# Reciprocal roots of the norms by one GpSimd power, weight splits and normed rows moved between VectorE, ScalarE and GpSimd, in a transformer of two parts on one core

## The chip, the cores and the metric

The kernel runs on one core of one Trainium2 chip. A core has five engines with queues of their own: PE (TensorE, matrix products), DVE (VectorE), ACT (ScalarE), POOL (GpSimd) and SP (SyncE, which here only issues loads). The metric is the time of one execution on the device in microseconds (us), lower is better; the median of the runs is compared.

## The reference

256 tokens of width 1024 go through two blocks. The first has two layers, each a feed-forward, a mixer of four attentions and a second feed-forward, with a layer norm behind each. The second has a convolution, an attention and two expert layers, with root-mean-square norms between them. Cut to what the change touches:

```python
def layer_norm(x, g, b):
    mu = jnp.mean(x, -1, keepdims=True)
    var = jnp.mean(jnp.square(x - mu), -1, keepdims=True)
    return (x - mu) * lax.rsqrt(var + LN_EPS) * g + b

def rms_norm(x, g):
    return x * lax.rsqrt(jnp.mean(x * x, -1, keepdims=True) + RMS_EPS) * g

for l in range(2):
    x = layer_norm(ALPHA * x + 0.5 * swiglu(x, ffn1...), ln1_g[l], ln1_b[l])
    x = layer_norm(ALPHA * x + hybrid_mixer(x, w_in[l], ...), ln2_g[l], ln2_b[l])
    x = layer_norm(ALPHA * x + 0.5 * swiglu(x, ffn2...), ln3_g[l], ln3_b[l])
# second block
h = h + conformer_conv(rmsnorm(h, a_norm_g))        # with a layer norm inside
h = h + peer(rmsnorm(h, f_norm_g[0]))
h = h + diff_attention(rmsnorm(h, b_norm_g), ...)   # with an rmsnorm for each of 8 heads
h = h + peer(rmsnorm(h, f_norm_g[1]))
out = rmsnorm(h, final_norm_g)
```

Each mixer has a norm of its inputs `mla_norm` and one behind each of its four groups.

## The kernel before

Activations lie transposed, features on the 128 partitions and tokens along the row, in tiles of 128x256. Every product with large weights is made of three matmuls, `mm3`: a number is split into a rounded high part and the rest (`wh` and `wl` of the weights, `xh` and `xl` of the activations), and high x high, low x high and high x low are summed in PSUM.

`weights` streams weights from DRAM through a ring: SP loads 128x1024 (`w`, four buffers), ACT rounds 128x512 of it to `wh` (L396), and the engine named by the string `self.lo` subtracts it, `wl = w - wh` (L398): `v` is DVE, `g` POOL, and longer strings are cycled. `wh` and `wl` have six buffers each; one feeds four steps of twelve matmuls. A buffer comes free when PE has done with it, so ACT's and DVE's or POOL's next instruction waits on PE, and PE on them.

A layer norm is put off. `project` leaves the unnormed rows (`x`, and `z` scaled by the gain) and their sums. The next stage starts with products on the unnormed `z` (its *head*: six chunks of the mixer's input, or four pairs of a feed-forward), and behind the first of them `factors` makes the norm: PE sums over the features (L300, L301), DVE makes mean and variance (L304 to L306), `newton` the reciprocal root, DVE the shift (L308), and PE spreads both over the partitions by transposes (`spread`, L445). PE's rows run in one order, so it stands at the spread until `newton` is done. Then `finish` makes the normed rows chunk by chunk, eight chunks: DVE multiplies and adds (L324, L325), ACT makes `xh` (L328) while POOL makes `x` (L329) from the same `lnt`, and DVE makes `xl` of both (L330). `newton` is eleven small DVE instructions, each reading the one before: two integer steps (L434, L435) and three rounds of three (L437 to L439).

It is called 30 times: in six layer norms' `factors`, in two `mla_norm`, eight `group_out` (behind each of a mixer's groups), five `rms_factor`, one in `conformer` and eight in the attention's heads (`step_N`).

The strings are `HEAD_LO = 'g'` (the heads of mixers and feed-forwards), `MIX_LO` and `OUT_LO` `'ggv'` (the rest of a mixer, and its output product), `'v'` for feed-forwards. The second block has strings of its own, in which POOL has most splits.

The order of instructions on each engine is set when the kernel is built, by a scheduler that follows a model of the times; engines then run their rows strictly in that order.

Of the kernel before, what the change touches and what calls it, by code (L numbers as in the profile page):

```python
# [15 lines left out]
U32 = mybir.dt.uint32  # L16
I32 = mybir.dt.int32
AF = mybir.ActivationFunctionType
ALU = mybir.AluOpType
# [12 lines left out]
HEAD_LO = 'g'  # L32
HEAD_AT = 1
MIX_LO = ('ggv', 'ggv')
OUT_LO = ('ggv', 'ggv')
# [249 lines left out]
class Rows:  # L285
# [8 lines left out]
    def factors(self, k):  # L294
# [12 lines left out]
        r = k.newton(v)  # L307
# [7 lines left out]
    def finish(self, k):  # L315
# [6 lines left out]
        for c in range(DC):  # L322
            q = k.tl(k.w1, [128, T], "lnt")
            nc.vector.tensor_tensor(q, xp[:, c], ps[:, 0], op=ALU.mult)  # L324
            nc.vector.tensor_tensor(q, q, ps[:, 1], op=ALU.add)  # L325
            if self.out is None:
                h, l = [a[:, :T] for a in self.xs[c]]
                nc.scalar.activation(h, q, AF.Identity, bias=b[:, c:c + 1], scale=g[:, c:c + 1])  # L328
                nc.gpsimd.tensor_scalar(o[:, c], q, g[:, c:c + 1], b[:, c:c + 1], op0=ALU.mult, op1=ALU.add)  # L329
                nc.vector.tensor_tensor(l, o[:, c], h, op=ALU.subtract)  # L330
            elif LN_H[c] == "s":
                nc.scalar.activation(o[:, c], q, AF.Identity, bias=b[:, c:c + 1], scale=g[:, c:c + 1])
            else:
                nc.gpsimd.tensor_scalar(o[:, c], q, g[:, c:c + 1], b[:, c:c + 1], op0=ALU.mult, op1=ALU.add)
# [12 lines left out]
class Kernel:  # L347
    def __init__(self, ctx, nc, tc, I):
# [9 lines left out]
        nc.vector.memset(self.ones, 1.0)  # L358
        self.col = self.tl(gp, [128, 3], "col")
# [69 lines left out]
    def newton(self, v):  # L429
# [3 lines left out]
        a = self.tl(self.wk, [128, 8], "na", bufs=4)[:v.shape[0], :v.shape[1]]  # L433
        nc.vector.tensor_scalar(y.bitcast(U32), v.bitcast(U32), 1, None, op0=ALU.logical_shift_right)  # L434
        nc.vector.tensor_scalar(y.bitcast(I32), y.bitcast(I32), -1.0, float(0x5f3759df), op0=ALU.mult, op1=ALU.add)  # L435
        for _ in range(3):
            nc.vector.tensor_tensor(a, v, y, op=ALU.mult)  # L437
            nc.vector.scalar_tensor_tensor(a, a, -0.5, y, op0=ALU.mult, op1=ALU.mult)
            nc.vector.scalar_tensor_tensor(y, a, 1.5, y, op0=ALU.add, op1=ALU.mult)  # L439
# [294 lines left out]
    def group_out(self, grp, o):  # L734
# [9 lines left out]
        r = self.newton(ss)  # L744
# [80 lines left out]
    def mla_norm(self, x):  # L825
# [16 lines left out]
        r = self.newton(t)  # L842
# [356 lines left out]
    def rms_factor(self, s2, t0):  # L1199
# [15 lines left out]
        r = self.newton(v)  # L1215
# [6 lines left out]
    def conformer(self, z, ss):  # L1222
# [62 lines left out]
        r = self.newton(v)  # L1285
# [29 lines left out]
    def attention(self, zk, ss):  # L1315
# [104 lines left out]
        def step_N(hd, n):  # L1420
# [8 lines left out]
            r = self.newton(q)  # L1429
# [289 lines left out]
```

## Time and profile before

| | us |
|---|---|
| median of three runs | 3370.47 |
| the three runs | 3356.43, 3370.47, 3370.92 |
| profiled execution | 3374.15 |
| its span, first to last instruction | 3372.3 |
| PE, DVE, ACT, POOL busy | 3205.0, 2399.8, 1650.9, 1190.2 |
| mean granted clock of PE | 0.963 |

PE is busy for 95% of the span, so the reading starts at PE's waits and at the stretches where its clock was granted at half. The first block takes the first 1230 us: feed-forward, mixer, feed-forward up to 625 us, and the same again. A head follows at about 200, 420, 625, 826 and 1035 us.

### The profile page before, as it was taken

How to read it: one execution, taken by the hardware profiler on the slowest of the kernel's cores; microseconds unless marked ns; L12 is line 12 of the kernel's file. 1: busy time of each engine (PE TensorE's matmuls, PEld its weight loads, DVE VectorE, ACT ScalarE, POOL GpSimd, SP SyncE). 2: the span in 40 equal slices, each digit the busy share in tenths (PEclk: the TensorE clock that was granted, in tenths of full speed). 3: DMA queues.
4: the chain of work that ended last, by engine and by line, in shares of the span. 5: the costliest groups of instructions: out<-in, count | busy, mean ns of one | idle time of the engine just before them, and what ended most of it. 6: DMA issues, size and time to landing. Idle time of an engine off the chain costs nothing.

```text
span 3372.3 us, 70124 instructions
## 1 busy us (share of the span) xinstructions
PE 3205.0 (95%) x27035; PEld 3082.0 (91%) x27035; DVE 2399.8 (71%) x5664; ACT 1650.9 (49%) x3361; POOL 1190.2 (35%) x958
## 2 busy tenths in 40 slices
PE   8989999999999999879999999999988999999998
PEld 8987799999778988879999999999887999999898
DVE  5666576766658579893797548956899397755965
ACT  5555355555535552545444454455454545445444
POOL 0053220303413000565444444344357544444443
PEclk9998799999889999989999999999998999999999
DMA  7642156565205653335444554454344545455454
GB/s 240 183 144 91 45 163 181 165 190 171 82 32 160 184 171 127 121 119 163 151 157 140 168 175 143 141 174 157 102 132 131 185 152 172 156 177 170 132 182 138
DMA packets 140863, 503.16 MB, mean 149 GB/s; under 512 B 17328, under 2 KB 19632, under 8 KB 139888
## 3 DMA queue, kind: packets, MB, share of 16 engines
q1 hardware_dynamic: 137104, 496.06, 46.6%
q8 instruction: 212, 3.47, 0.4%
q10 hardware_dynamic: 3328, 2.36, 0.2%
q14 instruction: 123, 1.01, 0.1%
q0 software_dynamic: 96, 0.26, 0.0%
HBM read 496.36 MB, written 1.05 MB: 147 GB/s over the span
## 4 chain that ended last, share of the span: by engine, by line
PE 51%; DVE 17%; issue 2%; ACT 0%; POOL 0%; DMA 0%; SPq 0%; DVEq 0%; ACTq 0%; POOLq 0%
PE A L420 7%; PE A L421 7%; PE A L422 7%; PE D L420 7%; PE D L422 7%; PE D L421 7%; DVE A L1503 2%; DVE two L1498 2%; DVE wl L398 1%; PE C L1507 1%; PE B L1246 1%; PE C L420 1%; PE C L421 1%; PE C L422 1%; DVE room L1604 1%
## 5 line engine op out<-in xcount | busy, mean ns | idle before, releaser
L396 ACT ACTIVATE wh<-w 128x512 fp32r<-128x512 f32 x1856 | 1152.9, 626 | 1313.7 <-PE A L421 513.4
L398 POOL TENSOR_TENSOR wl<-w,wh 128x512 fp32r<-128x512 f32 x774 | 1069.4, 1389 | 1622.5 <-ACT wh L396 1167.9
L398 DVE TENSOR_TENSOR wl<-w,wh 128x512 fp32r<-128x512 f32 x1082 | 764.3, 708 | 522.4 <-ACT wh L396 482.1
L420 PE MATMUL A<-xh,wh 128*128 128x256 f32 (+2 forms) x1912 | 558.8, 294 | 21.3 <-ACT wh L396 8.7
L421 PE MATMUL A<-xl,wh 128*128 128x256 f32 (+2 forms) x1912 | 556.6, 292 | 9.3 <-DVE xl L330 5.8
L422 PE MATMUL A<-xh,wl 128*128 128x256 f32 (+2 forms) x1912 | 555.1, 291 | 2.8 <-POOL wl L398 2.8
L420 PE MATMUL D<-xh,wh 128*128 128x256 f32 (+2 forms) x1664 | 481.3, 289 | 4.8 <-ACT wh L396 4.4
L422 PE MATMUL D<-xh,wl 128*128 128x256 f32 (+2 forms) x1664 | 477.9, 287 | 7.2 <-DVE wl L398 4.2
L421 PE MATMUL D<-xl,wh 128*128 128x256 f32 (+2 forms) x1664 | 477.9, 287 | 2.1 <-DVE xl L330 2.0
L420 PEld LDWEIGHTS A<-xh,wh 128*128 128x128 f32 x1912 | 370.4, 194 | 25.6 <-ACT wh L396 8.9
L421 PEld LDWEIGHTS A<-xl,wh 128*128 128x128 f32 x1912 | 371.5, 194 | 12.6 <-DVE xl L330 8.0
L422 PEld LDWEIGHTS A<-xh,wl 128*128 128x128 f32 x1912 | 372.6, 195 | 3.8 <-POOL wl L398 3.4
L421 PE MATMUL A<-rr,wh 128*128 128x272 f32 (+1 forms) x1152 | 333.4, 290 | 2.3 <-DVE rr L1196 2.2
L422 PE MATMUL A<-rr,wl 128*128 128x272 f32 (+1 forms) x1152 | 334.2, 290 | 1.1 <-POOL wl L398 1.1
L420 PE MATMUL A<-rr,wh 128*128 128x272 f32 (+1 forms) x1152 | 333.8, 290 | 0.0
L420 PE MATMUL D<-rr,wh 128*128 128x272 f32 (+1 forms) x1152 | 333.4, 289 | 0.0
L422 PE MATMUL D<-rr,wl 128*128 128x272 f32 (+1 forms) x1152 | 333.3, 289 | 0.0
L421 PE MATMUL D<-rr,wh 128*128 128x272 f32 (+1 forms) x1152 | 331.9, 288 | 0.0
L422 PEld LDWEIGHTS D<-xh,wl 128*128 128x128 f32 x1664 | 317.9, 191 | 9.7 <-DVE wl L398 5.6
L420 PEld LDWEIGHTS D<-xh,wh 128*128 128x128 f32 x1664 | 317.9, 191 | 6.7 <-ACT wh L396 5.5
L421 PEld LDWEIGHTS D<-xl,wh 128*128 128x128 f32 x1664 | 317.9, 191 | 3.4 <-DVE xl L330 3.1
L421 PEld LDWEIGHTS A<-rr,wh 128*128 128x128 f32 x1152 | 220.2, 191 | 2.8 <-DVE rr L1196 2.7
(482 smaller groups left out, 6775.2 us busy)
## 6 DMA issues: line engine op xcount, KB each, us to landing
w<-in_u_dram SPq DMA_DIRECT2D x256, 512.0 KB, 3.5
w<-in_v_dram SPq DMA_DIRECT2D x256, 512.0 KB, 3.8
w<-in_ffn_w_dram SPq DMA_DIRECT2D x240, 512.0 KB, 4.1
w<-in_win_f_dram SPq DMA_DIRECT2D x32, 512.0 KB, 3.6
w<-in_f_wq_dram SPq DMA_DIRECT2D x32, 512.0 KB, 3.5
w<-in_ffn_w_dram SPq DMA_DIRECT2D x32, 384.0 KB, 3.2
w<-in_pw_dram SPq DMA_DIRECT2D x24, 512.0 KB, 3.7
w<-in_w_out_dram SPq DMA_DIRECT2D x16, 512.0 KB, 3.7
```

The source lines that it names most:

```text
L396: nc.scalar.activation(h, s, AF.Copy)
L398: (nc.vector if eng == "v" else nc.gpsimd).tensor_tensor(l, s, h, op=ALU.subtract)
L420: mm(ps, wh, xh, start=start, stop=False)
L421: mm(ps, wh, xl, start=False, stop=False)
L422: mm(ps, wl, xh, start=False, stop=stop)
L1246: mm(pc, d[:, k], u[:, k:k + T2], start=k == 0, stop=k == n - 1)
L1498: nc.vector.tensor_tensor(two, self.key[:, None].to_broadcast([128, 4, 128, 2]), row(1, 128), op=ALU.is_equal)
L1503: nc.vector.tensor_tensor(A[:, i], one, row(2 + i, n), op=ALU.mult)
L1507: mm(ps[:, k], two[:, k // 2, :, k % 2], A[:, i, k // 2, :, k % 2], start=i == 0, stop=i == 1)
L1604: nc.vector.tensor_tensor(c[:, o:o + (b - a) * n].rearrange("p (a b) -> p a b", b=n), r.v[0][:, hd, a:b][:, :, None].to_broadcast([128, b ...
```

## The change

`newton` becomes `rsqrt`, one POOL instruction, `v ** -0.5` against a small constant tile. In the heads, in mixers and their output products all splits `wl` are made by DVE. In `finish`, ACT makes `x` (with gain and bias) and then `xh` as a rounded copy of it; POOL has nothing to do there. Lines from 358 on move by up to four.

```diff
-HEAD_LO = 'g'
+HEAD_LO = 'v'
-MIX_LO = ('ggv', 'ggv')
-OUT_LO = ('ggv', 'ggv')
+MIX_LO = ('v', 'v')
+OUT_LO = ('v', 'v')
...
-        r = k.newton(v)
+        r = k.rsqrt(v)
...
-                nc.scalar.activation(h, q, AF.Identity, bias=b[:, c:c + 1], scale=g[:, c:c + 1])
-                nc.gpsimd.tensor_scalar(o[:, c], q, g[:, c:c + 1], b[:, c:c + 1], op0=ALU.mult, op1=ALU.add)
+                nc.scalar.activation(o[:, c], q, AF.Identity, bias=b[:, c:c + 1], scale=g[:, c:c + 1])
+                nc.scalar.activation(h, o[:, c], AF.Copy)
                 nc.vector.tensor_tensor(l, o[:, c], h, op=ALU.subtract)
...
+        self.half = self.tl(gp, [128, 8], "half")
+        nc.gpsimd.memset(self.half, -0.5)
...
-    def newton(self, v):
+    def rsqrt(self, v):
         y = self.tl(self.wk, [128, 8], "ny", bufs=4)[:v.shape[0], :v.shape[1]]
-        a = self.tl(self.wk, [128, 8], "na", bufs=4)[:v.shape[0], :v.shape[1]]
-        nc.vector.tensor_scalar(y.bitcast(U32), v.bitcast(U32), 1, None, op0=ALU.logical_shift_right)
-        nc.vector.tensor_scalar(y.bitcast(I32), y.bitcast(I32), -1.0, float(0x5f3759df), op0=ALU.mult, op1=ALU.add)
-        for _ in range(3):
-            nc.vector.tensor_tensor(a, v, y, op=ALU.mult)
-            nc.vector.scalar_tensor_tensor(a, a, -0.5, y, op0=ALU.mult, op1=ALU.mult)
-            nc.vector.scalar_tensor_tensor(y, a, 1.5, y, op0=ALU.add, op1=ALU.mult)
+        nc.gpsimd.tensor_tensor(y, v, self.half[:v.shape[0], :v.shape[1]], op=ALU.pow)
         return y
```

The built programs show how rows move. First DVE in the head of layer 0's mixer, from the statistics of the layer norm on (`lnst`); before, with the first round of `newton` (`ny`, `na`):

```order
L304 COPY lnst_2638<-B_2633 128x4
L305 TENSOR_TENSOR lnst_2638<-lnst_2638 128x2
L306 SCALAR_TENSOR_TENSOR lnst_2638<-lnst_2638 128x2
L434 TENSOR_SCALAR ny_2642<-lnst_2638 128x2
L435 TENSOR_SCALAR ny_2642<-ny_2642 128x2
L437 TENSOR_TENSOR na_2643<-lnst_2638,ny_2642 128x2
L438 SCALAR_TENSOR_TENSOR na_2643<-na_2643,ny_2642 128x2
L439 SCALAR_TENSOR_TENSOR ny_2642<-na_2643,ny_2642 128x2
```

and after, on DVE at the same place:

```order
L400 TENSOR_TENSOR wl_2763<-w_2760,wh_2762 128x512
L304 COPY lnst_2640<-B_2635 128x4
L305 TENSOR_TENSOR lnst_2640<-lnst_2640 128x2
L306 SCALAR_TENSOR_TENSOR lnst_2640<-lnst_2640 128x2
L400 TENSOR_TENSOR wl_2767<-w_2760,wh_2766 128x512
L308 SCALAR_TENSOR_TENSOR lnst_2640<-lnst_2640,ny_2644 128x2
L400 TENSOR_TENSOR wl_2798<-w_2795,wh_2797 128x512
```

Before, two more rounds of three and L308 follow with no split between; now splits stand around the statistics, and L308 waits for POOL's `ny` with splits behind it.

POOL at that place; before, the last splits of the head alternate with the normed rows:

```order
L398 TENSOR_TENSOR wl_2811<-w_2804,wh_2810 128x512
L398 TENSOR_TENSOR wl_2917<-w_2914,wh_2916 128x512
L329 TENSOR_SCALAR x_1758<-lnt_2840,vec_6_93 128x256
L398 TENSOR_TENSOR wl_2954<-w_2951,wh_2953 128x512
L329 TENSOR_SCALAR x_1758<-lnt_2846,vec_6_93 128x256
```

and after, on POOL (`ISA` is the configuration of POOL's code; before it stands ahead of POOL's first split):

```order
L991 COPY acc_2879<-const_97 128x128 x2
L435 ISA
L435 TENSOR_TENSOR ny_2644<-lnst_2640,half_69 128x2
L601 TENSOR_TENSOR turn_2889<-turn_2889,const_97 128x256
L602 TENSOR_TENSOR m_478_2888<-m_478_2888,turn_2889 128x256
L890 TENSOR_TENSOR z_3480<-m_478_2888,small_101 64x240
```

POOL has no split left in the head: the power stands alone between the mixer's constants and the first rotary product.

DVE at the mixer's `mla_norm` (`mst` is its sum), before:

```order
L434 TENSOR_SCALAR ny_3038<-mst_3036 128x4
L398 TENSOR_TENSOR wl_3194<-w_3191,wh_3193 128x512
L603 STREAM_SHUFFLE turn_3065<-p_3057 128x256
L604 TENSOR_TENSOR iq_522_3064<-p_3057,const_95 128x256
L435 TENSOR_SCALAR ny_3038<-ny_3038 128x4
L437 TENSOR_TENSOR na_3039<-mst_3036,ny_3038 128x4
L398 TENSOR_TENSOR wl_3292<-w_3285,wh_3291 128x512
```

and after, on DVE:

```order
L837 TENSOR_SCALAR mst_3027<-D_3020 128x4
L344 TENSOR_TENSOR p_3037<-p_3037,lnt_3040 128x256
L400 TENSOR_TENSOR wl_3174<-w_3171,wh_3173 128x512
L599 STREAM_SHUFFLE turn_3045<-p_3037 128x256
L600 TENSOR_TENSOR iq_521_3044<-p_3037,const_97 128x256
L400 TENSOR_TENSOR wl_3178<-w_3171,wh_3177 128x512
L840 TENSOR_SCALAR mrq_3031<-ny_3029 128x2
```

Before, other work stands between the steps of `newton`; now only the use of its result (L840) is left, behind two splits and the rotary steps.

On PE, the number of matmuls between a norm's sums and its spread falls: from 49 to 37 in the mixers' heads (to 40 in the feed-forwards' heads), and from 62 to 31 in `mla_norm`. PE's rows also shift by a few places within the mixers, the conformer and the attention; in the feed-forwards behind their heads and in both expert layers behind their routing they stand as before. On SP two loads change places. POOL has 644 splits instead of 774, DVE 1212 instead of 1082; from the first of the expert layers on, `wl` is made where it was.

## Rows read from the trace of the kernel before

**Rows 1.** Page, part 1: busy us (share of the span) and instructions

```profile
PE 3205.0 (95%) x27035; PEld 3082.0 (91%) x27035; DVE 2399.8 (71%) x5664; ACT 1650.9 (49%) x3361; POOL 1190.2 (35%) x958
```

**Rows 2.** Waits of PE, whole run: us in total, times, longest us

```profile
PE B L445 <- DVE ny L439: 26.4, 10, 4.4
...
PE A L421 <- DVE xl L330: 5.8, 7, 1.1
...
PE B L300 <- DVE s L586: 3.3, 2, 1.9
PE A L421 <- DVE xl L580: 3.2, 2, 1.6
...
PE B L445 <- DVE cst L1286: 3.0, 1, 3.0
PE A L420 <- ACT sb L594: 3.0, 2, 1.5
```

**Rows 3.** Timeline of DVE, first layer norm: start, us, instruction

```profile
207.81 1.22 DVE L434 TENSOR_SCALAR ny<-lnst 128x2 uint32<-128x2 uint32 x1
...
214.02 0.16 DVE L439 SCALAR_TENSOR_TENSOR ny<-na,ny 128x2 f32<-128x2 f32 x1
```

**Rows 4.** Timeline of POOL in the same head

```profile
203.97 7.61 POOL L398 TENSOR_TENSOR wl<-w,wh 128x512 fp32r<-128x512 f32 x6
...
219.82 1.30 POOL L398 TENSOR_TENSOR wl<-w,wh 128x512 fp32r<-128x512 f32 x1 [2.73 <-ACT wh L396]
221.10 0.56 POOL L329 TENSOR_SCALAR x<-lnt,vec 128x256 f32<-128x256 f32 x1
```

**Rows 5.** Timeline of DVE, the last layer norm, POOL idle

```profile
1227.85 0.17 DVE L434 TENSOR_SCALAR ny<-lnst 128x2 uint32<-128x2 uint32 x1
...
1229.82 0.16 DVE L439 SCALAR_TENSOR_TENSOR ny<-na,ny 128x2 f32<-128x2 f32 x1
```

**Rows 6.** Timeline of DVE, layer 0's `mla_norm`

```profile
246.01 0.16 DVE L434 TENSOR_SCALAR ny<-mst 128x4 uint32<-128x4 uint32 x1
...
255.64 0.16 DVE L439 SCALAR_TENSOR_TENSOR ny<-na,ny 128x4 f32<-128x4 f32 x1
```

**Rows 7.** Splits, line 398, POOL (196 to 420 us), DVE (465 to 600): ns min/median/max

```profile
L398 POOL TENSOR_TENSOR wl<-w,wh x46: 1090/1292/2095, 195.8 to 418.6; 128x512 fp32r<-128x512 f32 x43, 128x424 fp32r<-128x424 f32 x3
...
L398 DVE TENSOR_TENSOR wl<-w,wh x97: 417/693/695, 465.1 to 599.4; 128x512 fp32r<-128x512 f32 x91, 128x256 fp32r<-128x256 f32 x6
```

**Rows 8.** Stretches: us; PE, PEld, DVE, ACT, POOL busy (instructions); PE's clock; DMA

```profile
400.00:425.00 25.00, 21.21 (x154) 20.40 (x153) 22.10 (x36) 14.35 (x31) 18.62 (x13) 0.91 0.45 137
425.00:465.00 40.00, 36.35 (x271) 35.04 (x270) 33.00 (x84) 26.42 (x51) 16.85 (x16) 0.93 0.49 145
```

**Rows 9.** Short stretches behind PE's waits at a spread, columns as before

```profile
215.60:219.00 3.40, 3.40 (x18) 3.40 (x17) 3.24 (x9) 1.12 (x2) 0.55 (x1) 0.50 0.07 6
219.00:222.40 3.40, 3.40 (x31) 3.40 (x30) 1.76 (x8) 2.60 (x5) 2.58 (x3) 1.00 0.40 122
256.50:263.30 6.80, 6.80 (x28) 4.90 (x27) 3.16 (x8) 3.72 (x6) 1.89 (x3) 0.50 0.25 78
...
1038.20:1041.60 3.40, 3.40 (x17) 3.40 (x18) 1.89 (x9) 1.23 (x2) 0.00 (x0) 0.50 0.09 34
```

**Rows 10.** Groups by line, whole run: busy us, mean ns, idle before

```profile
L329 POOL TENSOR_SCALAR x<-lnt,vec 128x256 f32<-128x256 f32 x40 | 33.7, 844 | 24.4 <-DVE lnt L325 20.3 <-PE A L421 3.5 <-PE A L422 0.5
...
L412 ACT ACTIVATE hh<-silu 128x256 fp32r<-128x256 f32 x88 | 35.5, 404 | 3.1 <-DVE silu L549 3.0
```

**Rows 11.** Groups of POOL by line and shape, whole run, columns as before

```profile
L605 POOL TENSOR_TENSOR turn<-turn,const 128x256 f32<-128x256 f32 x20 | 15.6, 778 | 28.4 <-DVE turn L603 28.4
...
L406 POOL COPY const<-silu 128x1 f32<-128x1 f32 x2 | 0.4, 187 | 93.2 <-DVE silu L549 93.2
```

**Rows 12.** Line 398 at 70 to 80 us: POOL's configuration, ns min/median/max

```profile
L398 POOLq MODIFY_POOL_CONFIG  x2: 1/3/5, 73.4 to 73.5; - x2
```

**Rows 13.** Waits of PE, 1380 to 2600 us, columns as in rows 2

```profile
PE B L445 <- DVE ny L439: 2.5, 2, 1.8
```

More of the change, by code (lines that the diff above doesn't have):

```diff
@@ L743, in group_out @@
         nc.vector.tensor_scalar(ss, ss, 1.0 / 256, 1e-6, op0=ALU.mult, op1=ALU.add)
-        r = self.newton(ss)
+        r = self.rsqrt(ss)
         y = self.tl(self.mx, [128, 2, T], "y", bufs=2)
@@ L841, in mla_norm @@
         nc.vector.tensor_scalar(t, st, 1e-6, None, op0=ALU.add)
-        r = self.newton(t)
+        r = self.rsqrt(t)
         rq = self.tl(mx, [128, 2], "mrq")
@@ L1214, in rms_factor @@
         nc.vector.tensor_scalar(v, st, 1e-6, None, op0=ALU.add)
-        r = self.newton(v)
+        r = self.rsqrt(v)
         ps = self.bank("B", T2 - t0)
@@ L1284, in conformer @@
         nc.vector.scalar_tensor_tensor(v, e2, 1e-6, v, op0=ALU.add, op1=ALU.subtract)
-        r = self.newton(v)
+        r = self.rsqrt(v)
         nc.vector.scalar_tensor_tensor(nmr, mean, -1.0, r, op0=ALU.mult, op1=ALU.mult)
@@ L1428, in step_N @@
             nc.vector.scalar_tensor_tensor(q, ss, 1.0 / 128, q, op0=ALU.mult, op1=ALU.add)
-            r = self.newton(q)
+            r = self.rsqrt(q)
             o = new_o()
```

## Prediction

> **What bounds the kernel now.** I read the page first: PE is busy 95% of the span [rows 1], so nothing is to be had but from PE's waits and from stretches in which its clock is granted at half. The view of PE's waits comes next. Its longest line is the spread of a norm's factors, which waits for `newton` on DVE: 26.4 us in ten waits, and 3.0 us in the conformer's norm (cst) [rows 2]. The waits for the splits of normed rows (xl L330), for an evacuation behind them (sb), and for the sums and splits of the mixer's output product (s L586, xl L580) are 5.8, 3.0, 3.3 and 3.2 us.
>
> The timelines tell why `newton` is slow. With POOL idle its eleven steps take 1227.85 to 1229.98, 2.1 us [rows 5]. In the first layer norm they take 207.81 to 214.18, 6.4 us: steps on two numbers per partition that last 0.16 or 0.17 us there last 1.2 us here [rows 3], and just then POOL has six splits in a row [rows 4] of 1.3 us each. So a small DVE step waits for a whole POOL split, again and again. In `mla_norm` it is 246.01 to 255.80, 9.8 us [rows 6]. Behind a wait PE pays once more: in 215.6 to 219.0 its clock is granted at 0.50 (1.2 GHz) and 18 matmuls run, in the next 3.4 us at 1.00 (2.4 GHz) 31 [rows 9].
>
> **The change part by part.** *The power.* It takes eleven DVE steps out and puts one POOL step on 2 to 4 numbers per partition in, with a hand-over to POOL and one back. No row shows a power. Below it is bounded by POOL's copy of one column, 0.19 us, and by a two-input POOL instruction of 256 columns, 0.78 us [rows 11], of 512 columns 1.29 us [rows 7]: a line through these two meets zero columns at 0.27 us. Above there is no row, since a power may be a long routine; I bound it by what `newton` took at its worst, 9.8 us. I take 1.0 us: nearest to the copy and the 0.27 us, with room for the function itself and for waiting behind a DVE split of 0.69 us [rows 7], which now stands beside it on DVE. The price moves nothing while it is covered. PE has 37 matmuls between sums and spread in a mixer's head, 40 in a feed-forward's; at 31 in 3.4 us [rows 9] that is 4.1 and 4.4 us. The chain in it is three small DVE steps, the power and L308, 0.8 us and the power; so a power of up to 3.3 us stops nobody. In `mla_norm` 31 matmuls give 3.4 us against 0.2 us and the power: up to 3.2 us.
>
> Ten plus one waits are 29.4 us [rows 2]. Three stand where PE has nothing between sums and spread (the last layer norm, the conformer, the final norm), and POOL is idle there: each waits about as long as `newton` and the steps around it, some 2.7 us by [rows 5] and 3.0 in the conformer's row, together 8.4 us, and each gains 2.1 - 1.0 - 0.2 for two hand-overs = 0.9, **-2.8 us**. Of the other eight, 21 us, two (2.5 us [rows 13]) are before expert layers, where POOL's queue is full of splits and the power stands among them: half of it goes. Six are in heads and `mla_norm` and are covered, 18.5 us. Together **-20 us**. In the mixers' groups and the attention's heads a shorter root lies beside other matmuls of PE; I count nothing there. In the attention the power is queued between the two rotary steps of a key on POOL (L1341, L1342), so the key waits for it; a step of 1 us ahead of the next scores is covered by the products of the same head, and costs up to 8 x 1 us if it is not.
>
> *The clock.* Five stretches at half clock follow those six waits, from 215.6 (3.4 us) and 256.5 (6.8 us) to 1038.2 us (3.4 us), 24 us in all [rows 9]. At half clock half is lost, 12 us, if PE had matmuls ready; behind `mla_norm` (28 matmuls in 6.8 us) it partly had not. **-8 us**.
>
> *The splits.* 130 of 128x512 go from POOL to DVE. On DVE one lasts 0.69, on POOL 1.29 us [rows 7], so DVE gets 90 us over both layers and loses 16 times `newton` of the first block, and the stretching. Whether it fits is seen in the tightest stretch, the output product: DVE is busy 22.1 of 25.0 us there and POOL's 13 splits would add 9.0 [rows 8], 6 us too many if DVE's own steps stay as they are. But part of these 22.1 us is waiting for POOL as in rows 3: eight steps stretched by some 0.7 to 1.1 us would make the room. In the next head it is 33.0 of 40 and eight of POOL's 16 instructions are splits (the others are L329), 8 x 0.69 = 5.5 [rows 8], which fits. I take that the waits for s L586 and xl L580, 6.5 us [rows 2], lose 2.5, **-2.5 us**, and that the fuller, single DVE queue gives new waits of 1 us in each of five heads and one more in the output products: **+6 us**. Behind L308, which waits for the power, splits stand in DVE's queue; six buffers of splits hold them off PE.
>
> *The normed rows.* POOL's 40 steps of 0.84 us (L329) go; ACT gets 40 rounded copies, 0.40 us each [rows 10], 16 us in all, beside PE. For one chunk `xl` now comes behind two ACT steps, where before ACT and POOL ran side by side: some 0.2 us later, but the whole row of chunks starts 4 to 6 us earlier. Of the waits for xl L330 and sb, 8.8 us [rows 2], I take half, **-5 us**, and **+1 us** for ACT.
>
> The sum: -20 - 2.8 - 8 - 2.5 + 6 - 5 + 1 = -31 us on the profiled execution of 3374.15 us (span 3372.3): 3343. That execution lies 3.7 us above the median of the runs; against the median, 3370.5, I say 3341.
>
> One rule of the Trainium skill speaks against the power. POOL switches from a split to a TENSOR_SCALAR within 0.02 us [rows 4], and its configuration row takes 5 ns, over 100 us ahead of the head's splits [rows 7, 12]; no row here shows a load of code. The skill (GPSIMD Engine Reference, Instruction dispatch) says that the first call of a freshly loaded kernel pays about 6 us (5.95 measured) that no instruction shows; paid once it would make the first head's spread some 1 us late, the sum -30, and paid at each return to the power it is the slow power below.
>
> **The rivals.** *More of the clock* (14%): in the mixers PE's matmuls follow short DVE and ACT steps in turn, and their clock is granted at half, as in 256.5 to 263.3, where 28 run in 6.8 us [rows 9]. Without POOL's splits these steps are shorter. If six more such stretches over both mixers come at full clock, that is 6 x 3.4 = 20 us more: 3321. Against it: no row shows PE waiting there by name.
>
> *DVE becomes the bound* (16%): the stretching is not given back, since DVE's splits now stand in front of the same small steps. Then the two output products lack 6 us each, the five heads behind layer norms some 2 us each, half of the clock's 8 us comes, and nothing of the -5, -2.5 and +6: -20 - 2.8 - 4 + 12 + 10 = -5, 3366 against the median. For it: the 22.1 of 25 us; against it: one split is half as long on DVE as on POOL.
>
> *The waits go, the clock does not* (6%): the half-clock stretches come behind whatever short wait is next. -31 + 8 + 4 = -19: 3352.
>
> *A slow power* (7%), the one that ends slower. If one takes 6 us, the six covered places wait 6 x 2.7 = 16 us, about what they waited; the three bare ones lose 4.1 each, 12 us; the eight groups of the mixers, with half of 3.9 us each on the way, 16 us; and nothing of the clock or the chunks is gained. About +25: 3396. It decides from about 4.5 us on, where 6 x 1.2 + 3 x 2.6 + 8 x 1.2 = 25 us eat what the sum gains from the waits and half of the rest. For it only that no row excludes it; against it that POOL's rows grow by 2 ns a column [rows 7, 11] and this has two to four.
>
> *The roots are no bound* would be the case where the change does not do what it says; the ten waits exclude it, as each names `newton`.
>
> **How the numbers follow.** The forecast, 3341, has 57%. Its own bounds: with the power at 0.3 us and all of the half-clock 12 us back, 3334; with a power at 3 us (3 x 2 us more) and +12 of new waits, 3353. A range that leaves out the slow power and the outer half of the clock's rival is 3315 to 3367; it takes in DVE as the bound. 0.5% is about what a measurement of this kernel can tell from no change, 17 us: faster is below 3353.6. To it go the forecast, the clock's rival and half of the third (57 + 14 + 3) and a little of DVE's (2): 76%. Within 0.5%: 14 + 3 = 17%. Slower: 7%.
>
> **What would show it.** In the profile of the changed kernel: PE's wait for `ny` at the spread below 8 us in total, and only where PE has nothing between; a POOL row of 128x2 of about 1 us; DVE's L305, L306, L308 at 0.16 us; no half clock at 215.6 and 256.5; DVE in the output product at 20 to 23 of 25 us. It is wrong if POOL's 128x2 row lasts over 3.3 us, if PE's waits for `wl` and `xl` from DVE grow by more than 12 us, or if the granted clock of the mixers' middle falls.

## The result

| | before | after |
|---|---|---|
| median of the runs, us | 3365.65 | 3312.70 |
| all runs, us | 3356.43 to 3370.92 | 3310.59 to 3317.83 |
| profiled span, us | 3372.3 | 3312.0 |
| mean granted clock of PE | 0.963 | 0.970 |

The changed kernel takes 0.984 of the time before (95% interval 0.9811 to 0.9868), 53 us less by the medians. The forecast was 3341, a gain of 29, and the range 3315 to 3367 ends 2 us above what came: the sign is right, the size is not. One execution of the run mix_back, told below, took 7458 us, over twice the others, and stands in no ratio.

Page of after, part 1 (busy us, share of the span, instructions), against [rows 1]:

```profile
PE 3182.8 (96%) x27035; PEld 3058.0 (92%) x27035; DVE 2335.8 (71%) x5464; ACT 1663.4 (50%) x3401; POOL 1006.8 (30%) x819
```

Waits of PE in after, whole run (us in total, times, longest us), against [rows 2]:

```profile
PE D L423 <- DVE xl L330: 3.6, 8, 0.8
...
PE A L423 <- DVE xl L330: 2.6, 4, 0.7
...
PE B L441 <- POOL ny L435: 2.5, 2, 1.5
...
PE B L300 <- DVE s L582: 1.9, 1, 1.9
...
PE B L441 <- DVE cst L1282: 1.9, 1, 1.9
```

The spread's wait fell from 29.4 us (26.4 and 3.0) to 4.4, and stands only at the three places without cover, at 1185.8, 1299.5 and 3304.7 us. Of the output product's waits, 3.3 us for `s` and 3.2 for `xl`, the one for `xl` is gone and that for `s` is down to 1.9. PE's waits for `wl` from DVE are 0.5 us in all.

The power, line 435 of after by its input (count; ns min/median/max; first and last start in us):

```profile
L435 POOL TENSOR_TENSOR ny<-ss,half x8: 695/701/707, 298.5 to 963.7; 128x2 f32<-128x2 f32 x8
...
L435 POOL TENSOR_TENSOR ny<-lnst,half x6: 695/696/711, 208.0 to 1185.1; 128x2 f32<-128x2 f32 x6
...
L435 POOL TENSOR_TENSOR ny<-mst,half x2: 1141/1144/1147, 237.8 to 824.5; 128x4 f32<-128x4 f32 x2
L435 POOL TENSOR_TENSOR ny<-cst,half x1: 1007/1007/1007, 1298.3 to 1298.3; 68x4 f32<-68x4 f32 x1
```

DVE's timeline in the first head of after (start, us, instruction, idle before), against [rows 3]:

```profile
206.76 0.69 DVE L400 TENSOR_TENSOR wl<-w,wh 128x512 fp32r<-128x512 f32 x1 [0.43 <-ACT wh L398]
207.37 0.15 DVE L304 COPY lnst<-B 128x4 f32<-128x4 f32 x1
207.56 0.16 DVE L305 TENSOR_TENSOR lnst<-lnst 128x2 f32<-128x2 f32 x1
207.76 0.16 DVE L306 SCALAR_TENSOR_TENSOR lnst<-lnst 128x2 f32<-128x2 f32 x1
208.34 0.69 DVE L400 TENSOR_TENSOR wl<-w,wh 128x512 fp32r<-128x512 f32 x1 [0.42 <-ACT wh L398]
208.94 0.15 DVE L308 SCALAR_TENSOR_TENSOR lnst<-lnst,ny 128x2 f32<-128x2 f32 x1
```

Stretches of after: the two behind the first spreads, against [rows 9], then the output product, against [rows 8] (us; PE, PEld, DVE, ACT, POOL busy with instructions; PE's clock; DMA):

```profile
211.20:214.60 3.40, 3.40 (x30) 3.40 (x30) 2.69 (x7) 2.26 (x5) 0.00 (x0) 1.00 0.65 203
242.50:249.30 6.80, 6.80 (x46) 5.18 (x44) 5.07 (x13) 6.01 (x10) 0.00 (x0) 1.00 0.60 195
...
383.70:408.40 24.70, 24.68 (x207) 24.47 (x207) 21.01 (x50) 15.81 (x34) 0.00 (x0) 1.00 0.55 171
```

Both stretches right behind these spreads are at full clock now. Half clock is still granted in the same mixer, at 238.7 to 242.2 us and at 262.6 to 269.4. In the output product DVE makes 50 instructions in 21.0 us, where [rows 8] has 36 in 22.1. The two stretches do not hold the same rows (PE runs 207 matmuls in the one and 154 in the other), so the steps themselves tell more. Two groups of DVE's splits `xl` between 200 and 1240 us, those of the normed rows (L330) and those of the output product (L580, in after L576), first of before, then of after (count; busy us, mean ns; idle before):

```profile
L330 DVE TENSOR_TENSOR xl<-x,xh 128x256 fp32r<-128x256 f32 x40 | 26.8, 669 | 6.2 <-ACT xh L328 4.0 <-POOL x L329 1.6
L580 DVE SCALAR_TENSOR_TENSOR xl<-x,vec,xh 128x256 fp32r<-128x256 f32 x33 | 22.6, 686 | 0.5 <-ACT xh L579 0.5
```

```profile
L330 DVE TENSOR_TENSOR xl<-x,xh 128x256 fp32r<-128x256 f32 x40 | 16.9, 429 | 1.5 <-ACT xh L329 1.2
...
L576 DVE SCALAR_TENSOR_TENSOR xl<-x,vec,xh 128x256 fp32r<-128x256 f32 x33 | 16.0, 485 | 0.5 <-ACT xh L575 0.5
```

The same steps are about a third shorter, and such time is where the room for the moved splits came from.

Where the time went, by the start of PE's sums for each layer norm (L300), from the traces; two runs told below stand beside it:

| stage, us | before | power_only | splits_only | after |
|---|---|---|---|---|
| mixer of layer 0 | 217.1 | 225.5 | 198.0 | 203.1 |
| second feed-forward of layer 0 | 201.1 | 197.8 | 195.9 | 190.6 |
| first feed-forward of layer 1 | 199.0 | 192.6 | 196.1 | 192.2 |
| mixer of layer 1 | 206.7 | 202.7 | 201.5 | 202.3 |
| second feed-forward of layer 1 | 198.3 | 192.9 | 190.8 | 189.7 |
| second block up to the last spread | 2139.3 | 2118.7 | 2135.9 | 2121.5 |

The mixers' stages hold a large share of half clock: in layer 0's it is 75, 93, 41 and 51 us. With half of that taken off, the most that it can have cost, the four take 180, 179, 178 and 178 us, and in layer 1 the same sum gives 177 to 180. So what a mixer's stage gains or loses in this table is mostly its clock, and the feed-forwards' stages and the second block are the better guide.

From PE's first row to its last, the gaps in which neither a matmul nor a weight load of PE runs fell from 152.8 to 114.8 us, 38 us. The time at half clock, worked out from the mean clock and span of each, fell from 249 to 199 us, worth 25 us of full-clock work at most. The forecast had 22.8 us of spreads, 0.5 of other waits net, and 8 of clock.

### The profile page after: what moved, and what is told of

Same layout as the page of the kernel before. It is cut to its first block, busy times and chain, and to the rows that moved or that the text cites. A ratio compares the mean times of both kernels' runs of the same rounds, so it can differ in the third digit from the quotient of the medians.

```text
span 3312.0 us, 69651 instructions
## 1 busy us (share of the span) xinstructions
PE 3182.8 (96%) x27035; PEld 3058.0 (92%) x27035; DVE 2335.8 (71%) x5464; ACT 1663.4 (50%) x3401; POOL 1006.8 (30%) x819
## 4 chain that ended last, share of the span: by engine, by line
PE 75%; DVE 18%; issue 5%; ACT 2%; POOL 0%; DMA 0%; ACTq 0%; SPq 0%; POOLq 0%; DVEq 0%
PE A L422 10%; PE A L423 10%; PE A L424 10%; PE D L422 9%; PE D L423 9%; PE D L424 9%; PE C L422 3%; PE C L423 3%; PE C L424 3%; DVE two L1494 2%; DVE A L1499 2%; DVE wl L400 2%; PE B L758 2%; PE C L1503 1%; DVE room L1600 1%
## 5 line engine op out<-in xcount | busy, mean ns | idle before, releaser
L400 DVE TENSOR_TENSOR wl<-w,wh 128x512 fp32r<-128x512 f32 (+1 forms) x1212 | 859.9, 713 | 550.0 <-ACT wh L398 524.4
L400 POOL TENSOR_TENSOR wl<-w,wh 128x512 fp32r<-128x512 f32 x644 | 888.3, 1385 | 978.1 <-ACT wh L398 938.5
```

The source lines that it names most:

```text
L400: (nc.vector if eng == "v" else nc.gpsimd).tensor_tensor(l, s, h, op=ALU.subtract)
```

## The experiments

Two theories. **The roots**: what is gained comes from PE's waits for the root and the half clock behind them. **POOL's splits**: a POOL split holds up every small DVE step while it runs; the root in [rows 3] is only where PE shows it by name. Times below are medians; a difference in brackets is worked out from the ratio to the kernel before of the same runs, with its 95% interval.

### One part at a time

**power_only**, the kernel before with this alone:

```diff
-        r = k.newton(v)
+        r = k.rsqrt(v)        # in all six places
```

> The kernel before with the power alone: roots on POOL, splits and normed rows as before. The roots' theory (what the change gains comes from PE's waits for the root and the half-clock stretches behind them) expects most of the change's gain of about 53 us: 35 to 45 us below the kernel before, and the three spreads without cover at 1 to 2 us. The theory of POOL's splits (what slows DVE's small steps is POOL's splits, and it does so in every step, not only in the root's) expects about half, 20 us, because the power must now wait in POOL's queue behind splits of 1.29 us and the other small steps stay stretched. The prediction's own terms for this part alone are -20 - 2.8 - 8 = -31 us.

Measured: 3337.9, ratio 0.9922 (0.9896 to 0.9947), so -26 us (-35 to -18). Near the prediction's -31, but the table shows it in other places: the two mixers together lose 4 us, with 93 us at half clock in the first where before had 75, and the second block gains 21 where 3 to 4 were counted.

**splits_only**, the kernel before with this alone:

```diff
-HEAD_LO = 'g'
+HEAD_LO = 'v'
-MIX_LO = ('ggv', 'ggv')
-OUT_LO = ('ggv', 'ggv')
+MIX_LO = ('v', 'v')
+OUT_LO = ('v', 'v')
```

> The kernel before with the 130 splits of heads, mixers and output products on DVE alone; the roots stay on DVE in eleven steps, the rows on ACT and POOL. The theory of POOL's splits expects 30 to 40 us below the kernel before: with POOL out of the way the eleven steps take about 2.1 us in the heads, which PE's matmuls cover, so that PE's six covered waits for ny (18.5 us) go without a power. The roots' theory expects 5 to 15 us: the eleven steps now stand in DVE's queue among 0.69 us splits and still hold PE. The prediction's terms for the splits alone are -2.5 + 6 = +3.5 us.

Measured: 3337.1, ratio 0.9925 (0.99 to 0.995), so -25 us (-34 to -17). The prediction's +3.5 is refuted. Of the expectation of POOL's splits, 30 to 40 us, the lower end is within the interval; the roots' 5 to 15 is not. Waits of PE at the spread in this run (columns as above), with `newton` still on DVE, and part 1 of its page:

```profile
PE B L445 <- DVE ny L439: 9.7, 6, 2.8
...
PE B L445 <- DVE cst L1286: 3.0, 1, 3.0
```

```profile
PE 3182.4 (96%) x27035; PEld 3064.2 (92%) x27035; DVE 2395.4 (72%) x5794; ACT 1651.3 (50%) x3361; POOL 1023.1 (31%) x828
```

Two things are to be seen. The wait for `ny` fell from 26.4 us to 9.7 without any power: in the heads and `mla_norm` from 18.7 to 0.7, and the other 9.0 stand at the last layer norm and in the second block. And DVE does 130 more splits, 90 us by [rows 7], yet is busy 4 us less than in [rows 1]. One thing stays open: with the splits moved the scheduler also set some of PE's rows in another order, as it did in most runs told here, and what that is worth was not measured by itself.

**rows_only**, the kernel before with this alone:

```diff
-                nc.scalar.activation(h, q, AF.Identity, bias=b[:, c:c + 1], scale=g[:, c:c + 1])
-                nc.gpsimd.tensor_scalar(o[:, c], q, g[:, c:c + 1], b[:, c:c + 1], op0=ALU.mult, op1=ALU.add)
+                nc.scalar.activation(o[:, c], q, AF.Identity, bias=b[:, c:c + 1], scale=g[:, c:c + 1])
+                nc.scalar.activation(h, o[:, c], AF.Copy)
```

> The kernel before with the normed rows by ACT alone (POOL's 40 steps of 0.84 us go). The prediction's term is -5 + 1 = -4 us, both theories agree: 0 to -6 us. If it is over 10 us the rows are a cause of their own.

Measured: 3360.6, ratio 0.9984 (0.9962 to 1.0005), so -5 us (-13 to +2). As forecast. The three ratios multiply to 0.983, the change's is 0.984: within intervals of some 9 us on each part they add up, and the splits are the one that the sum had wrong.

**no_power**, the changed kernel with `newton` back:

> The changed kernel with the root back on DVE in eleven steps (splits and rows as changed). The roots' theory expects 10 to 20 us below the kernel before, that is 35 to 45 us above the changed one. The theory of POOL's splits expects 35 us or more below the kernel before, and that what is left to the power, some 15 us, comes from the second block, where POOL still has splits (the spreads at about 1230, 1350 and 3365 us and those of the expert layers).

Measured: 3329.3, ratio 0.9891 (0.9861 to 0.9921), so -37 us (-47 to -27), and 17 us above the changed kernel by the medians. That is what the theory of POOL's splits expected (35 or more below the kernel before, some 15 left for the power); the roots' 10 to 20 below lies outside the interval.

**head_back** and **mix_back**, the changed kernel with one group of splits back on POOL:

```diff
-HEAD_LO = 'v'
+HEAD_LO = 'g'
```

> The changed kernel with the splits of the heads on POOL again. The theory of POOL's splits expects 10 to 18 us above the changed kernel: in five heads the small DVE steps of the norm last 1.2 us again and the power waits in POOL's queue behind a split, some 2 to 3.5 us per head. By the prediction's terms (nothing for the heads' splits but new waits of 1 us in each of five heads that would go) it is 0 to 5 us below the changed kernel.

```diff
-MIX_LO = ('v', 'v')
-OUT_LO = ('v', 'v')
+MIX_LO = ('ggv', 'ggv')
+OUT_LO = ('ggv', 'ggv')
```

> The changed kernel with two of three splits of the mixers and of their output products on POOL again. The theory of POOL's splits expects 10 to 20 us above the changed kernel, of which 6 us at the output products (PE's waits for the sums s and the splits xl there come back) and the rest between mla_norm and the output product. By the prediction's terms (-2.5 for the output product, +1 for a fuller queue) it is 2 us above.

Measured: 3324.6 (ratio 0.9886, 0.9869 to 0.9902) and 3321.5 (0.9881, 0.9861 to 0.9901), so 12 and 9 us above the changed kernel by the medians, 15 and 14 by the ratios. Beside the power the splits are worth some 21 to 29 us by the sum of the two. For the heads the prediction's term (0 to 5 us below the changed kernel) is refuted, and in the trace the second feed-forwards, 5 and 7 us longer, show it. For the mixers' group the interval of the ratio overlaps that of the changed kernel at its edge, and the trace shows both mixers together as long as in after (405 us), so against the prediction's +2 this run alone decides little. The theory of POOL's splits fits splits_only, no_power and head_back; the next runs test its mechanism.

### Is it POOL's reading?

Each of these has splits_only's work on DVE and PE, and something of POOL's beside each moved split (`MIX_LO` and `OUT_LO` are 'xxv', `HEAD_LO` is 'x'). In pool_beside and beside_fill all rows of DVE and PE also stand in the order of splits_only; in beside_copy they stand otherwise from some 220 us on.

**pool_beside**:

```diff
+                if eng == "x":
+                    nc.gpsimd.tensor_tensor(self.idle[:, :j * m], s, h, op=ALU.subtract)
```

> The kernel of the run splits_only (all splits of heads, mixers and output products on DVE, roots in eleven DVE steps), and beside each of the 130 moved splits POOL makes the same subtraction into a tile that nobody reads. So DVE's and PE's work is that of splits_only, and POOL is as busy as before the change. If POOL's splits cost time because they hold up DVE's small steps while they run (rows 3 and 6 of before), the gain of splits_only, 31.6 us, is lost or more than lost: 3358 to 3385. If they cost time because PE waits for a split that takes 1.29 us in place of 0.69, the gain stays: 3337 to 3345.

Measured: 3429.3, ratio 1.0208 (1.0181 to 1.0236), 92 us above splits_only: worse than the worst expected. DVE's timeline in the first head, and part 1 of the page:

```profile
211.04 0.15 DVE L304 COPY lnst<-B 128x4 f32<-128x4 f32 x1
211.22 1.07 DVE L305 TENSOR_TENSOR lnst<-lnst 128x2 f32<-128x2 f32 x1
212.33 0.16 DVE L306 SCALAR_TENSOR_TENSOR lnst<-lnst 128x2 f32<-128x2 f32 x1
212.52 1.15 DVE L436 TENSOR_SCALAR ny<-lnst 128x2 uint32<-128x2 uint32 x1
...
214.19 1.24 DVE L437 TENSOR_SCALAR ny<-ny 128x2 int32<-128x2 int32 x1
```

```profile
PE 3220.8 (94%) x27035; PEld 3094.3 (90%) x27035; DVE 2513.8 (73%) x5794; ACT 1652.3 (48%) x3361; POOL 1217.1 (36%) x958
```

The same 5794 DVE instructions take 118 us more, 0.91 us for each POOL row, and PE's wait for `ny` is 41.1 us. It left open whether POOL's late rows, which also hold `w` and `wh`, had a share in it.

**beside_fill**:

```diff
+                    nc.gpsimd.tensor_copy(self.idle[:, 0:1], h[:, 0:1])
+                    nc.gpsimd.memset(self.idle.bitcast(F32), 0.0)
+                    nc.gpsimd.memset(self.idle.bitcast(F32), 0.0)
```

> As pool_beside, but in place of each subtraction beside a split POOL copies one column of wh and then fills a tile of 512 columns twice with a constant. POOL is busy about as long (a copy of a column 0.19 us, a fill of 384 columns 0.42 us on the page of after, so an estimate of 0.19 + 2 x 0.55 = 1.3 us against 1.55), stands at the same places and holds wh just as it did, but not w, and reads next to nothing. If what cost 92 us in pool_beside is that POOL is busy and late and so holds buffers, this costs as much, some 60 to 90 us above splits_only (3337). If it is POOL's reading of two tiles from SBUF against DVE's, it costs little: 3337 to 3350, and DVE's small steps stay at 0.16 us.

Measured: 3346.5, ratio 0.995 (0.9926 to 0.9973), 9 us above splits_only, with intervals that overlap. Groups of DVE between 200 and 1240 us (count; busy us, mean ns; idle before), first of pool_beside, then of beside_fill, and beside_fill's page:

```profile
L398 DVE TENSOR_TENSOR wl<-w,wh 128x512 fp32r<-128x512 f32 x465 | 378.1, 818 | 175.1 <-ACT wh L396 161.2 <-PE A L423 5.1 <-PE D L423 3.7
...
L305 DVE TENSOR_TENSOR lnst<-lnst 128x2 f32<-128x2 f32 x5 | 4.4, 871 | 0.2
```

```profile
L398 DVE TENSOR_TENSOR wl<-w,wh 128x512 fp32r<-128x512 f32 x505 | 349.6, 696 | 212.1 <-ACT wh L396 191.8 <-PE C L425 7.3 <-PE A L425 6.6
...
L305 DVE TENSOR_TENSOR lnst<-lnst 128x2 f32<-128x2 f32 x6 | 1.0, 161 | 0.2
```

```profile
PE 3191.5 (96%) x27035; PEld 3072.9 (92%) x27035; DVE 2401.6 (72%) x5794; ACT 1651.8 (49%) x3361; POOL 1201.5 (36%) x1218
```

POOL is as busy (1201.5 against 1217.1 us) and holds `wh` as before, but DVE's steps keep their 0.16 and 0.70 us, and DVE pays 6 us in place of 118. So what stretches DVE's steps is the reading of tiles by POOL, not its being busy. Whether `w`, which pool_beside holds longer and beside_fill does not, had a share in the 92 us of time is not shown.

**beside_copy**:

```diff
+                    nc.gpsimd.tensor_copy(self.idle[:, :j * m], s)
```

> As pool_beside, but beside each split POOL copies w (one input) in place of subtracting two tiles; it holds w as long as pool_beside did, wh not. If any POOL instruction on SBUF stops DVE's, the loss goes with POOL's busy time: 30 to 90 us above splits_only. If only two-input instructions do, 0 to 10 us above it, and DVE's small steps stay at 0.16 us.

Measured: 3361.8, ratio 0.9981 (0.9967 to 0.9996), 25 us above splits_only by the medians and 19 by the ratios. DVE is busy 2430.7 us, 35 more, 0.27 for each copy of 0.79 us. One input costs too, though less: L305 lasts 0.31 us on the mean. Whether DVE's steps explain all of the lost time is not settled, since the clock is lower too (the median over the runs is 0.9645 against splits_only's 0.971) and the rows stand in another order.

### What the power is worth

**power_second**, the changed kernel with the power in the second block only:

> The changed kernel with the power in the second block only (conformer, its norms, attention heads), eleven DVE steps in the first block and in its last layer norm. Against no_power (3329.3) it shows what the power is worth in the second block: by the prediction's terms two bare spreads of 0.9 us and two spreads before expert layers of 0.6 us, 3 us with nothing of the clock, so 3326; if each of these waits draws a stretch of half clock behind it, 10 to 16 us, so 3313 to 3319.

Measured: 3317.7, ratio 0.9876 (0.9853 to 0.9899), 12 us below no_power by the medians and 5 by the ratios, with intervals that overlap. So the times do not tell 3 us from 10 to 16. The traces tell one stretch better: from the sums of the last layer norm to the conformer's spread PE takes 123.9 to 124.8 us in all eight runs with `newton` there (before, splits_only, rows_only, no_power, all_v_newton and the three of the section before this) and 116.3 to 116.5 in all seven with one power there (after, power_only, head_back, mix_back, and route_v, all_v and all_v_turns, told below). There the power is worth 8 us, where PE's waits at the two spreads by name shrink by 2.4.

no_power and power_second have the same rows in the same order on PE and on DVE in the whole first block. The stretch of the first mixer's softmax in the one and in the other:

```profile
310.00:380.00 70.00, 70.00 (x280) 53.84 (x280) 32.82 (x149) 17.36 (x70) 1.78 (x2) 0.51 0.10 34
```

```profile
310.00:380.00 70.00, 66.54 (x355) 53.28 (x355) 39.56 (x170) 21.61 (x80) 1.79 (x2) 0.73 0.13 43
```

So one execution differs from another by the clock of a mixer, 280 or 355 matmuls in 70 us, with the same rows in the same order; the whole mixer of layer 0 takes 211.9 us in the one and 200.6 in the other. A difference of some 10 us in a mixer, read from one trace each, says nothing of a change.

**power_x4** and **power_x8**, the power written four or eight times in a row:

```diff
-        nc.gpsimd.tensor_tensor(y, v, self.half[:v.shape[0], :v.shape[1]], op=ALU.pow)
+        for _ in range(4):        # 8
+            nc.gpsimd.tensor_tensor(y, v, self.half[:v.shape[0], :v.shape[1]], op=ALU.pow)
```

> The changed kernel with each power written four times in a row, so a root on two columns takes 2.8 us in place of 0.70, on three or four columns 4.6 in place of 1.14. By the prediction's cover (3.3 us in heads and mla_norm, nothing for groups and attention heads) the five heads stay free, mla_norm waits 1.4 us twice, and the bare spreads pay all: the last layer norm 2.1, conformer 3.0, final norm 2.1, the two before expert layers half of 3: 13 us above the changed kernel, 3325. The rival is that the eight mixer groups and the eight attention heads have each root on the way, 16 x 2.1 = 34 us more, 3359.

> The changed kernel with each power written eight times in a row: 5.6 us for two columns, 9.1 for three or four. By the prediction's cover four mixer and feed-forward heads wait 2.3 us each, a fifth the same, mla_norm 5.9 twice, the bare spreads 4.9, 7 and 5 to 8, half of 8 at the two before expert layers: about 48 us above the changed kernel, 3361, that is about the kernel before, which would put the break-even near 6 us where the prediction said 4.5. If groups and attention heads have the root on the way it is 16 x 4.9 = 78 us more, 3439.

Measured: 3327.3 (ratio 0.9889, 0.9853 to 0.9924) and 3369.3 (1.0013, 0.9995 to 1.0031), 15 and 57 us above the changed kernel where 13 and 48 were expected. The rows of PE's waits for the root, of power_x4 and then of power_x8:

```profile
PE B L442 <- POOL ny L436: 8.4, 3, 3.7
...
PE B L442 <- DVE cst L1283: 5.2, 1, 5.2
```

```profile
PE B L442 <- POOL ny L436: 29.3, 8, 6.8
...
PE B L442 <- DVE cst L1283: 9.5, 1, 9.5
...
PE B L759 <- POOL ny L436: 0.9, 2, 0.5
...
PE B L947 <- POOL ny L436: 0.3, 1, 0.3
```

At 2.8 us a root no head waits at its spread; PE's gaps there are at the three bare spreads and once, not twice, at `mla_norm`, 1.33 us where 1.4 was expected. The norms before the expert layers wait for nothing. At 5.6 us two of the five heads wait, 2.65 us each where 2.3 was expected for all five, and `mla_norm` waits 1.1 and 2.6 us where 5.9 was expected twice. The mixers' groups are not free, which the names of these rows hide: the transposes behind the last group of each mixer wait for DVE's `y`, which needs the root, 1.0 us in after, 7.2 in power_x4 and 11.0 in power_x8.

```profile
PE C L746 <- DVE y L744: 1.0, 2, 0.5
```

```profile
PE C L747 <- DVE y L745: 7.2, 2, 4.7
```

```profile
PE C L747 <- DVE y L745: 11.0, 2, 5.5
```

So of the expected terms the bare spreads were right, the cover was met or better, and the nothing for groups was wrong. Eight powers come out at the kernel before, so the change would break even at about 5.6 us for two columns, not at 4.5.

### Going on

**route_v**, the changed kernel with

```diff
-ATT_LO = 'gvv'
+ATT_LO = 'v'
...
-        self.lo = "g"        # the expert layers' routing
+        self.lo = "v"
```

> A version that goes on: the changed kernel with the splits of the attention and of the expert layers' routing on DVE too. If a POOL split takes from DVE what it lasts (1.3 us for 0.7 of DVE's own), this gains even in the routing, where DVE is busy 95 of 95 us (1345 to 1440): about 100 splits on POOL in both stretches, so 5 to 15 us below the changed kernel. If DVE's own work is the bound there and POOL's runs beside it for free, it is 20 to 40 us slower.

**all_v**, with this as well:

```diff
-PEER_LO = 'gv'
+PEER_LO = 'v'
```

> The same with the expert layers' remaining splits, now alternating between POOL and DVE, on DVE alone. DVE is busy 85 of 140 us where the products with values run (2150 to 2290), and a further half of the splits there (26 x 0.7 = 18 us) fits; in the stretches with DVE's gates it may not. Expected within 10 us of the run route_v if POOL's splits cost DVE as much as its own; slower by 20 us or more if DVE is the bound in the gates.

Measured: 3264.2 (ratio 0.9715, 0.9676 to 0.9754) and **3236.4** (0.962, 0.9586 to 0.9655), 48 and 76 us below the changed kernel and far beyond what was expected. In the traces the 76 us are all in the second block, which falls from 2121.5 to 2046 us. A step of the routing in after and in all_v (line 1600; count; ns min/median/max), and all_v's page:

```profile
L1600 DVE TENSOR_TENSOR room<-room x66: 176/201/1314, 1345.3 to 2503.9; 128x48 f32<-128x48 f32 x33, 128x64 f32<-128x64 f32 x33
```

```profile
L1600 DVE TENSOR_TENSOR room<-room x66: 182/204/228, 1353.5 to 2494.3; 128x48 f32<-128x48 f32 x33, 128x64 f32<-128x64 f32 x33
```

```profile
PE 3161.7 (98%) x27035; PEld 3047.1 (94%) x27035; DVE 2467.2 (76%) x6108; ACT 1669.7 (52%) x3403; POOL 125.3 (4%) x175
```

DVE takes 644 splits more, 644 x 0.69 = 444 us, and is busy only 131 us more than in after. The other 313 us, 0.49 for each split, are what POOL's splits had cost DVE. Even in the routing, where DVE is never idle in after (102.3 of 102.3 us from 1342.7 us on), POOL's help was no help.

**all_v_turns** puts the rotary products and sums, and the splits `xl` of the routing, on DVE too:

> The version all_v (3236 us) with POOL's last two-input work on DVE as well: the rotary steps of mixers and attention (68 POOL rows of 0.7 to 1.1 us) and twelve splits xl of the routing. If each takes its time from DVE anyway, the change is worth its hand-overs: 3 to 12 us below all_v. If the rows run beside idle DVE, as the attention's gaps suggest, nothing or up to 5 us slower.

Measured: 3242.8, ratio 0.9638 (0.9617 to 0.966); not faster than all_v, and the intervals overlap. POOL rows of 0.8 us that stand beside idle DVE may stay.

**all_v_newton**, all_v with `newton` back:

> The version all_v (every split on DVE, 3236 us) with the root back in eleven DVE steps. If the root was slow only because POOL's splits stood in its steps, it now takes about 2.1 us plus the DVE splits between, PE covers it in heads and mla_norm, and only the five spreads without much cover pay, 1 to 2 us each: 5 to 12 us above all_v, 3241 to 3248. If the power is worth as much as on the kernel before (26 us by its ratio), it is 3262.

Measured: 3248.2, ratio 0.9646 (0.9627 to 0.9665), 12 us above all_v by the medians and 9 by the ratios, as the first of the two expectations; the intervals overlap, but the second expectation, 3262, lies above every run. PE's waits for `ny` and `cst` are 8.9 us there and 4.4 in all_v. Where no POOL split disturbs it, the root in eleven steps costs less than half of the 26 us that the power gained on the kernel before.

## Why the prediction was wrong, step by step

*PE's waits at the spread* (-20 and -2.8). Right in total and in place: 29.4 us became 4.4, under the 8 forecast. The bare places were priced too low, though: by the stretch told under power_second the last layer norm, the next norm and the conformer's are worth 8 us together, and the final norm's wait fell by 1.4 more.

*The price of the power* (1.0 us). Right: 0.70 for two columns, 1.14 for four; L305, L306 and L308 last 0.15 to 0.16 us, as forecast. Of the 6 us of a first call, the rule that the prediction took from the Trainium skill (GPSIMD Engine Reference, Instruction dispatch), no cost is seen here: the configuration stands at 203.1 us, the first power at 208.0, right behind L306, and PE waits for nothing at that spread. POOL was idle in those 4.9 us, so a cost paid in them would not show. By the prediction's own cover of 3.3 us, 6 us in the way of that spread would hold it by 2.7 and not by 1, an estimate with that page's figure.

*The slow power.* It did not come. power_x8 shows that its mechanism was right: at 5.6 us the bare spreads wait 18 us more, the heads, `mla_norm` and two more norms 16, the groups and the mixers' later products 11, in all 45 us, where the prediction had 44 for 6 us. Its point, 4.5 for about 5.6 us, was too low mainly because there was more to be eaten: it set the loss against a gain without the splits.

*The clock* (-8). The stretches right behind those spreads are gone, as forecast, though one of 6.8 us stands at 262.6 in the same mixer. The profiled executions differ by 25 us of work in this term, half of it in the long stretches in the middle of the mixers. There no_power and power_second show a swing of such size without any change of rows, so the share that belongs to the change stays open. Without these stretches the first block's half clock fell from 44 to 31 us, 7 us of work, near the 8 forecast. The second block is 18 to 21 us shorter in power_only and after, where its waits at spreads shrank by some 6 (from the 8.4 and 2.5 of the prediction to 4.4). Eight us of it repeat in every trace with one power, as told above; what the others are is not shown.

*The splits* (-2.5 + 6). **This is the step that failed**, and it accounts for the miss: +3.5 forecast, -25 (-34 to -17) measured alone, -21 to -29 beside the power. The forecast gain of 31 with -25 in place of +3.5 would have been 60, in which 18 us of waits stand twice, as told below; 53 came. Two sentences of the prediction did it. It took rows 3 as the trouble of `newton`, whose steps the change removes, and "DVE gets 90 us"; the stretching that DVE "loses" in return it left without a price for the whole. But steps of DVE are held up so all over the first block, the 128x256 splits `xl` of L330 (669 ns before, 447 in splits_only, 429 after) as well as the small ones. splits_only shows the balance: 90 us of splits more, and DVE 4 us less busy. And "new waits of 1 us in each of five heads" were made for a fuller queue that did not become fuller. In the output product DVE's 21.0 of 24.7 us lie within the 20 to 23 forecast, and there the prediction had even worked out that the stretching could make the room; it then carried only 2.5 us of it into the sum. The rival in which DVE becomes the bound failed for the same reason.

*More of the clock*, 3321, is the nearer number, but its mechanism is not shown. In splits_only both mixers are shorter (19 and 5 us), and 17 us of the first are half clock that fell from 75 to 41 us. But no_power, with the same splits on DVE, has 79 us of it and a first mixer of 211.9 us. So the clock of a mixer does not follow the splits from run to run.

*The power's sum.* power_only's -26 stands close to the -31 for spreads and clock, partly by luck: the second block gave more than its terms, the first less. And the terms were not independent as the sum took them: in the heads and `mla_norm` the splits alone take the wait for `ny` from 18.7 to 0.7 us, so most of the -20 could have been had without the power. That is why the power is worth 26 us on the kernel before and some 17 with splits and rows changed, as far as the intervals tell these apart.

*The last step of the sum* holds a slip: -31 on 3374.15 and 3.7 less for the median make 3339, not 3341. That is small beside the miss.

*The normed rows* (-5 + 1). Right within the interval: -5 (-13 to +2).

The Trainium skill has the rule that speaks of the splits, though no price for them (SBUF — State Buffer, Who interferes with whom): a VectorE instruction with two SBUF inputs contends with a GpSimd instruction that reads SBUF, not with one that only writes it, and whichever starts second blocks until the first has ended. By that rule pool_beside must cost and beside_fill must not. The traces agree: L305 lasts 0.87 us in the one and 0.16 in the other. An instruction of one input is affected as well: L437 lasts 1.24 us in pool_beside.

## What to carry to other kernels

Where one small DVE step in a trace lasts as long as a POOL instruction beside it, count that stretch for every DVE step with tiles in SBUF, over the whole kernel, before charging DVE for work moved to it: here a POOL split took 0.5 to 0.9 us of DVE's time and cost DVE 0.69 when it made it itself. An engine's busy time is then no measure of its room, since part of it is waiting for the other engine. A wait that a trace puts down to one engine can be another's work: the groups' roots showed under DVE's `y`. Before two parts of a change are added up, ask whether both remove the same wait.

## What was not expected of the hardware

- DVE's busy time holds its waiting for POOL: 118 us more for the same 5794 instructions when POOL reads two tiles beside them (0.91 us for each POOL row of about 1.55 us), 35 us when it copies one (0.27 for 0.79), 6 us when it only fills.
- A power of two to four numbers per partition on POOL lasts 0.70 to 1.14 us, repeated ones the same (medians 0.70 for two columns with one, four and eight in a row).
- The same rows in the same order on PE ran a mixer's softmax at a mean clock of 0.51 in one execution and 0.73 in another: 280 and 355 matmuls in 70 us.
- What a longer root costs is found only with the waits under another name: at the spreads PE's waits grew by 9 us with four powers and by 36 with eight, behind the groups' `y` by 6 and 10 more, and the time by 15 and 57. With four the waits make up the whole, with eight 46 of 57; where the other 11 went is not shown.
